# Gated MLP of a two-layer trunk: from a down-projection woven into the up-projection to two phases, with the down-projection in seven products over h kept in DRAM

## The chip, the cores and the metric

The kernel runs on one core of a Trainium2 chip. A core has five engines that run their own instruction lists side by side: TensorE (PE: matmuls, with weight loads, PEld, beside them), VectorE (DVE), ScalarE (ACT), GpSimd (POOL) and SyncE (SP, here only a queue of DMA transfers). They share an on-chip memory, SBUF; matmuls write to eight PSUM banks of 128 × 512 float32. The metric is the time of one execution on the device in microseconds (us): of the kernel before, the median of three runs is 2856.36 us (2855.16 to 2858.88).

## The reference

The reference is a trunk of two layers on x of 1024 positions and 1024 channels. Layer 0 mixes dilated attention with a short convolution, layer 1 is a retention layer; each is followed by a gated MLP with a causal convolution of width 3, which is what the change is about:

```python
def conv_glu_ffn(xn, w_up, conv_w, w_down):
    u = causal_dwconv(xn @ w_up, conv_w)      # 1024 -> 2 x 2816
    g, val = jnp.split(u, 2, axis=-1)
    return (jax.nn.silu(g) * val) @ w_down    # 2816 -> 1024

x = x + conv_glu_ffn(rms_norm(x, ffn_norm[l]), ffn_w_up[l], ffn_conv_w[l], ffn_w_down[l])
```

## The kernel before, in words

**Precision.** Every float32 operand of a large product is kept as a pair of fp32r tiles, high and low (`split`, L99 to L102: ACT casts the high half at L101, another engine subtracts it at L102), and each product is three matmuls (`PASSES`: high × high, high × low, low × high). Weights arrive by SP's queue in `raw` tiles of 128 × 512 (256 KB, L118), of which there are RAW = 3, and become pairs in `hl` tiles, HL = 6. One MLP phase reads the normed x, transposed, from `xc`, which holds the combinations of its halves that the seven products need.

**Up-projection.** The 2816 columns of each half of `w_up` are 22 column blocks of 128 (NFF = 22). `strassen` makes one block: gate and value columns together are a 2 × 2 block product done with seven products instead of eight (Strassen and Winograd). A product is 12 matmuls of 128 × 512 (4 along the contraction, 3 passes), a block 84. They use four PSUM banks x, y, wb, z, from the tags `b`; a `yield` stands behind each product. The weights of the seven products are three blocks of w (11, 12, 22) and four sums of blocks (s1 to s4): DVE adds s1 and s2 (L237, L238), POOL s3 and s4 (L239, L258) and POOL does all seven splits (L102). ACT copies banks out (L245, L261, L266, L272), DVE adds further banks to the copies (L250, L271, L273, L276). The product that comes sixth accumulates once more in bank x and must wait for the copy of x behind the fourth (L261).

**Convolution and gate.** `conv` takes the block's two tiles: ACT multiplies by the third tap (L724), DVE adds the two other taps (L727, two per tile), ACT takes silu (L731), DVE multiplies gate and value (L732), and h is split by ACT and POOL into a pair in SBUF.

**Down-projection.** `down` is a `sweep` over the eight tiles of 128 positions and two halves of the output channels: 16 accumulations of three matmuls each (L289), 48 in a block, and each is added to the residual x in `xb` by DVE (L294). So each of the 22 blocks adds its own share of the down-projection to `xb`: 1056 matmuls and 352 evictions a layer. They use four banks with the tag `o`.

**Order.** The order of emission is written by hand. In `ffn`, `MIX` says how many tiles of the down-projection of the block before are woven in behind each of the seven products of this block. The scheduler keeps the order of PE and may move instructions of the others by their dependencies. The next layer's norm, its transposes and the first block of the next phase (`first_block`, on half-width pieces in all eight banks) are woven by `PLAN` into the sweep of the last block.

Of the kernel before, what the change touches and what calls it, by code (L numbers as in the profile page):

```python
# [9 lines left out]
F32R = mybir.dt.float32r  # L10
# [11 lines left out]
AH = 8  # L22
EPS = 1e-6

RAW = 3
HL = 6

FILL = (1, 2)

PLAN = "s0 q0 s1 q1 r0 t0 s2 q2 c0 r1 t1 s3 q3 c1 r2 t2 c2 r3 h3 t3 c3 h4"  # L30
PLAN_LATE = "t0 c0 s2 q2 t1 s3 q3 c1 r2 t2 c2 r3 t3 h3 c3 h4"
# [37 lines left out]
def trunk(tc, a):  # L69
# [5 lines left out]
    def nm(s):  # L75
        uid[0] += 1
        return f"{s}_{uid[0]}"

    class Pool:


        def __init__(self, name, side="left", space=None):
            kw = {} if space is None else {"space": space}
            self.cm = tc.tile_pool(name=nm(name), bufs=1, side=side, **kw)
            self.p = self.cm.__enter__()

# [108 lines left out]
        for b, t in ((3, t1), (5, t3), (4, t2), (6, t4)):  # L195
            put(b, t, pool)

    def strassen(w, c1, c2, xc, fp, banks, out, spare=None):

        np_ = len(banks)
        width = HALF // np_
        helper = pool if np_ == 1 else dve

        def product(u, hl, b, first=True):
            for k in range(4):
# [16 lines left out]

        def weights(name, src, into=None):
            if name not in hl:
                hl[name] = hilo(src, into, helper)

        for n, bank in enumerate(banks):  # L230
            cols_, ps_ = slice(n * width, (n + 1) * width), n
            if n == 0:
                a11 = col_block(w, c1, 0)
                weights(11, a11)
                a21, a22 = col_block(w, c2, 0), col_block(w, c2, 1)
                s1, s2, s3 = s_tile(), s_tile(), s_tile()
                dve.tensor_tensor(s1, a21, a22, ALU.add)  # L237
# [3 lines left out]
                weights(12, a12)  # L241
                u1, u2 = fp.tile([P, T], "u", 4), fp.tile([P, T], "u", 4)
# [28 lines left out]
            dve.tensor_tensor(half(u2, 1), half(u2, 1), v(x), ALU.add)  # L271
            act.copy(half(u2, 0), v(x))  # L272
            dve.tensor_tensor(half(u2, 0), half(u2, 0), v(wb), ALU.subtract)  # L273
            yield
            product(z, hl["s4"], 2, False)
            dve.tensor_tensor(half(u1, 1), half(u1, 1), v(z), ALU.add)  # L276
# [372 lines left out]
    class Norming:  # L649


        def __init__(self, g):
            self.g = row_gains(g, [wk.tile([P, HALF], "s", 3) for _ in range(2)])
            self.r, self.rows, self.pts = {}, {}, {}

        def play(self, plan, xc=None, sweep=None, head=None):

            for what, n in plan.split():
                n = int(n)
                if what in "sh":
                    for _ in range(2 if what == "s" else n):
                        next(sweep if what == "s" else head)
                elif what == "q":
                    self.r[n] = [
                        inverse_rms(xb[:, t, :], wk.tile([P, T], "s", 3, mybir.dt.bfloat16)) for t in PAIRS[n]
                    ]
                elif what == "r":  # L670
                    self.rows[n] = [normed(xb[:, t, :], r, self.g, u_tile()) for t, r in zip(PAIRS[n], self.r[n])]
                elif what == "t":
                    self.pts[n] = [turn(xn, h, b_bank) for h in range(2) for xn in self.rows[n]]
                else:
                    combine(n, self.pts[n], xc, u_tile(), u_tile())

    def first_block(w, c1, c2, xc):

        us = []

        def spare():
            return h_tile().rearrange("p s (a n) -> p (s a) n", a=2)[:, :2, :]

        return strassen(w, c1, c2, xc, Both, (o_bank, b_bank), us, spare), us

    class Both:
        @staticmethod
# [6 lines left out]
    nrm.play(PLAN, xc, project((6,), ORDER, o_bank), head[0])  # L694


    def ffn(l, xc, head, tail):
# [13 lines left out]
        def wcol(k, j):  # L711
            return cc[:, 44 * k + j : 44 * k + j + 1]

        def conv(j, us, ranges):

            cs = u_tile(), u_tile()
            if len(ranges) == 1:
                h = h_tile()
                h = [h[:, :, :HALF], h[:, :, HALF:]]
            else:  # L720
                h = [wp.tile([P, 2, HALF], "hl", HL, F32R) for _ in ranges]
            for t0, t1 in ranges:
                for jj, u, c in ((NFF + j, us[1], cs[1]), (j, us[0], cs[0])):
                    act.mul(c[:, t0:t1], u[:, t0:t1], wcol(2, jj))  # L724
                    for d in (1, 2):
                        s0 = max(t0, d)
                        dve.scalar_tensor_tensor(  # L727
                            c[:, s0:t1], u[:, s0 - d : t1 - d], wcol(2 - d, jj), c[:, s0:t1], ALU.mult, ALU.add
                        )
                c = cs[0][:, t0:t1]  # L730
                act.activation(c, c, AF.Silu)  # L731
                dve.tensor_tensor(c, c, cs[1][:, t0:t1], ALU.mult)  # L732
                for i in range(t0, t1, HALF):
                    split(h[i // HALF][:, 0], h[i // HALF][:, 1], cs[0][:, i : i + HALF])
            return h

        def down(j, h, tiles, after=None):
            def lhs(s, t):
                return h[t // 4][:, s, t % 4 * P : (t % 4 + 1) * P]

            return sweep([lhs], [w_rows(w_down, j)], tiles, o_bank, after)

        d = iter(())
        for j in range(NFF):
            last = j == NFF - 1
            us = head[1] if j == 0 else []
            steps = head[0] if j == 0 else strassen(w_up, j * P, (NFF + j) * P, xc, Both, (b_bank,), us)
            for n, _ in enumerate(steps):
                for _ in range((MIX, LAST_MIX)[last][n]):
                    next(d, None)  # L750
            if j == 0:
                conv_columns()
            h = conv(j, us, ((0, HALF), (HALF, T)) if last else ((0, T),))
            run(d)
            if not last:
# [236 lines left out]
    def to_out(down):
        run(down(range(NT), lambda t: sync.dma_start(out=a["out"][0, t * P : (t + 1) * P, :], in_=xb[:, t, :])))

    ffn(1, xc, head, to_out)
    close_xc(0, 1, 6, 4, 3, 5, 2)
# [26 lines left out]
```

## Time and profile before

| | us |
|---|---|
| median of three runs | 2856.36 |
| the profiled execution | 2857.22 |
| its span, first to last instruction | 2855.4 |
| PE busy in it | 2743.8 |
| DVE busy | 1802.9 |
| POOL busy | 1553.9 |
| ACT busy | 1101.1 |

The mean granted TensorE clock of the execution is 0.983 of full. PE busy is not PE at its peak: matmuls overlap, so the time of one instruction is longer than the pace at which they follow. The program falls into these stretches (us from the span's start): layer 0's mixer to about 480, the first blocks of its MLP to 625, the steady MLP 625 to 1229, the way to layer 1 (1229 to 1308), the projections of the retention layer and its chunks (1308 to 2110), the way to the second MLP, its steady part 2216 to 2820, and the end. The trace's views by stretch, by line and by chain of waits are shown with the prediction, at the places that use them.

### The profile page before, as it was taken

To read this page: it belongs to the slowest core of one execution; us is meant where nothing else is said; L and a number is where in the kernel's file an instruction comes from. 1 tells how busy PE (TensorE), PEld (TensorE's weight loads), DVE (VectorE), ACT (ScalarE), POOL (GpSimd) and SP (SyncE) were. 2 spreads that over 40 slices of the span, in tenths; PEclk is the share of its full clock that TensorE was granted. 3 is DMA by queue.
4 is the path that set the end of the run, shared out by engine and by line. 5 is a ranking of instruction groups with operands and counts; after the bars stand their busy time and mean duration, and the time that the engine had idled before them with its cause. 6 is when DMAs were issued, how large, how long until landed. Compare 5 with 4: busy or idle time off the path is not lost.

```text
span 2855.4 us, 34163 instructions
## 1 busy us (share of the span) xinstructions
PE 2743.8 (96%) x12513; PEld 2208.3 (77%) x12513; DVE 1802.9 (63%) x2670; ACT 1101.1 (39%) x1860; POOL 1553.9 (54%) x1185
## 2 busy tenths in 40 slices
PE   8999999799999999979999999999997999999998
PEld 6877777578888888867888877788876888888886
DVE  4257665967767767784222224888777767767767
ACT  4355452443333333343333334323344433343342
POOL 6721113465665666546566665555555665665663
PEclk9999999899999999989999999999999999999999
DMA  4310002011111111103333335444221111111112
GB/s 153 103 42 26 24 31 89 23 57 56 48 49 59 49 48 56 49 22 103 112 111 100 109 109 189 147 145 154 83 70 53 48 50 58 49 48 57 51 49 78
DMA packets 214988, 210.84 MB, mean 74 GB/s; under 512 B 10368, under 2 KB 162340, under 8 KB 214820
## 3 DMA queue, kind: packets, MB, share of 16 engines
q1 hardware_dynamic: 207900, 183.49, 20.9%
q10 hardware_dynamic: 6920, 25.17, 2.2%
q8 instruction: 98, 1.61, 0.2%
q14 instruction: 70, 0.57, 0.1%
HBM read 179.26 MB, written 29.36 MB: 73 GB/s over the span
## 4 chain that ended last, share of the span: by engine, by line
PE 76%; DVE 11%; POOL 4%; issue 3%; DMA 3%; ACT 2%; SPq 0%; POOLq 0%; ACTq 0%; DVEq 0%
PE b L210 44%; PE o L289 17%; PE u L419 4%; PE n L368 2%; DVE xb L294 2%; POOL hl L102 2%; PE u L368 2%; PE pv L489 1%; DVE u L164 1%; PE u L289 1%; PE s L458 1%; DMA raw<-in_ret_wo 1%; PE pt L501 1%; DMA raw<-in_ffn_w_up 1%; DVE s L807 1%
## 5 line engine op out<-in xcount | busy, mean ns | idle before, releaser
L210 PE MATMUL b<-xc,hl 128*128 128x512 f32 (+1 forms) x5676 | 1333.1, 393 | 5.8 <-DVE xc L102 2.8
L210 PEld LDWEIGHTS b<-xc,hl 128*128 128x128 f32 x5676 | 1057.2, 189 | 260.0 <-DVE xc L102 3.5
L102 POOL TENSOR_TENSOR hl<-raw,hl 128x512 fp32r<-128x512 f32 x435 | 577.0, 1332 | 862.3 <-ACT hl L101 858.3
L294 DVE TENSOR_TENSOR xb<-xb,o 128x512 f32<-128x512 f32 x880 | 571.7, 683 | 306.3 <-PE o L289 303.5
L101 ACT CAST hl<-raw 128x512 fp32r<-128x512 f32 x444 | 274.2, 620 | 809.7 <-issue 289.2
L289 PE MATMUL o<-hl,h 128*128 128x512 f32 x2112 | 521.0, 398 | 15.4 <-DVE xb L294 11.6
L289 PEld LDWEIGHTS o<-hl,h 128*128 128x128 f32 x2112 | 400.6, 190 | 113.7 <-DVE xb L294 15.5
L102 POOL TENSOR_TENSOR hl<-s,hl 128x512 fp32r<-128x512 f32 x260 | 406.1, 1563 | 107.2 <-ACT hl L101 107.1
L727 DVE SCALAR_TENSOR_TENSOR u<-u,cc,u 128x1023 f32<-128x1023 f32 (+3 forms) x184 | 289.2, 1580 | 7.7 <-ACT u L724 4.9
L101 ACT CAST hl<-s 128x512 fp32r<-128x512 f32 x269 | 165.6, 617 | 89.5 <-PE b L210 40.5
L271 DVE TENSOR_TENSOR u<-u,b 128x512 f32<-128x512 f32 (+1 forms) x68 | 45.9, 675 | 208.6 <-issue 189.2
L419 PE MATMUL u<-xT,hl 128*128 128x512 f32 x576 | 171.2, 413 | 0.0
L237 DVE TENSOR_TENSOR s<-raw,raw 128x512 f32<-128x512 f32 x68 | 52.2, 768 | 137.3 <-DMA raw<-in_ffn_w_up 37.5
L258 POOL TENSOR_TENSOR s<-raw,s 128x512 f32<-128x512 f32 x65 | 126.9, 1953 | 5.1
L724 ACT ACTIVATE u<-u,cc 128x1024 f32<-128x1024 f32 (+1 forms) x92 | 102.0, 1115 | 55.8 <-DVE u L273 31.7
L239 POOL TENSOR_TENSOR s<-raw,raw 128x512 f32<-128x512 f32 x65 | 88.7, 1365 | 54.0 <-DMA raw<-in_ffn_w_up 45.6
L419 PEld LDWEIGHTS u<-xT,hl 128*128 128x128 f32 x576 | 98.2, 189 | 23.3 <-issue 9.3
L102 POOL TENSOR_TENSOR h<-u,h 128x512 fp32r<-128x512 f32 x84 | 106.7, 1290 | 0.0
L289 PE MATMUL o<-hl,ya 128*128 128x512 f32 x384 | 95.4, 397 | 3.7 <-DVE xb L294 3.7
L289 PEld LDWEIGHTS o<-hl,ya 128*128 128x128 f32 x384 | 71.2, 188 | 20.8 <-DVE xb L294 4.6
L102 POOL TENSOR_TENSOR xc<-u,xc 128x512 fp32r<-128x512 f32 x48 | 68.1, 1445 | 35.3 <-ACT xc L101 28.7
L732 DVE TENSOR_TENSOR u<-u,u 128x1024 f32<-128x1024 f32 (+1 forms) x46 | 54.4, 1183 | 49.9 <-ACT u L731 49.9
(183 smaller groups left out, 3040.8 us busy)
## 6 DMA issues: line engine op xcount, KB each, us to landing
raw<-in_ffn_w_up SPq DMA_DIRECT2D x176, 256.0 KB, 2.9
scr<-u ACTq DMA_DIRECT2D x48, 512.0 KB, 4.3
raw<-in_ffn_w_down SPq DMA_DIRECT2D x88, 256.0 KB, 2.7
raw<-in_even_w_in SPq DMA_DIRECT2D x72, 256.0 KB, 2.8
raw<-in_ret_wo SPq DMA_DIRECT2D x64, 256.0 KB, 2.7
xb<-in_x SPq DMA_DIRECT2D x16, 512.0 KB, 4.2
raw<-in_ret_wv SPq DMA_DIRECT2D x32, 256.0 KB, 4.1
raw<-in_ret_wg SPq DMA_DIRECT2D x32, 256.0 KB, 3.4
```

The source lines that it names most:

```text
L101: act.copy(hi, src)
L102: (eng or pool).tensor_tensor(lo, src, f(hi), ALU.subtract)
L210: pe.matmul(u, hl[:, ws, k * P : (k + 1) * P], xc[b][:, xs, k, cols_], start=(first and k == 0 and i == 0), stop=(k == 3 and i == 2), skip ...
L239: helper.tensor_tensor(s3, a11, a21, ALU.subtract)
L258: helper.tensor_tensor(s4, a12, s2, ALU.subtract)
L289: pe.matmul(o, lhs[j](ls, t), ws[j][hf][:, w, :], start=(j == 0 and i == 0), stop=(j == n - 1 and i == 2),)
L294: dve.tensor_tensor(xs, xs, o, ALU.add)
L368: pe.matmul(banks[t], xT[:, xs, k, t0 : t0 + P], hl[:, ws, :], start=(k == 0 and i == 0), stop=(k == KT - 1 and i == 2),)
L419: pe.matmul(u, hl(ws, k), xT[:, xs, k, hf * 512 : (hf + 1) * 512], start=(k == 0 and i == 0), stop=(k == KT - 1 and i == 2),)
L724: act.mul(c[:, t0:t1], u[:, t0:t1], wcol(2, jj))
L727: dve.scalar_tensor_tensor(c[:, s0:t1], u[:, s0 - d : t1 - d], wcol(2 - d, jj), c[:, s0:t1], ALU.mult, ALU.add)
L732: dve.tensor_tensor(c, c, cs[1][:, t0:t1], ALU.mult)
```

## The change

**Two phases.** In each MLP all 22 blocks of the up-projection run first, alone. h is no longer split in SBUF; each block's h (128 × 1024 float32, 512 KB) is stored to DRAM (`hs`, L901, on ACT's DMA queue), after the second product of the next block. The blocks take the four `b` and the four `o` banks by turns.

**Down-projection in seven products.** `down_steps` treats w_down and h as 2 × 2 blocks: h by halves of the 2816 channels and halves of the 1024 positions, w_down by halves of its rows and of its output channels. Groups 12, 56 and 37 each do two of the seven products: 11 steps (KH = 11) of 24 matmuls into all eight banks. Groups 4 and 4b do the last one in two halves, 11 steps of 6 matmuls each. That is 924 matmuls a layer and 28 evictions (L834). Rows of h are read back once, in group 12 (L735, two of 512 KB a step), and stay in SBUF; sums are formed in place (L758). The combination t4 goes to DRAM from group 4 (`ts`, L809) and is read again, with a quarter of h, into raw tiles in group 4b (L814, L815). Loads run four steps ahead (LOADS), splits two (AHEAD).

**Engines.** In a full-width block only the splits of 11, 12 and 22 stay on POOL. The other four splits and the sums s3 and s4 move to DVE, and so do all splits and sums of the down phase.

**Around it.** RAW goes from 3 to 5, HL from 6 to 7; tiles wait for a tile's reuse, not a slot's neighbours (`reuse_waits="tile"`); the gains of a norm have a tag of their own; the first block hands its steps out by one more yield. `PLAN_DOWN` weaves the norm and the first block of the retention layer into groups 4 and 4b of MLP 0, with the position tiles in another pairing (`lay=1`). At the end `to_out` stores tiles of the output between the steps of groups 4 and 4b.

Lines move: L102 becomes L110, L210 becomes L220, L250 L264, L261 L275, L271 L285, L272 L286, L276 L290, L289 L303 (attention and retention only), L724 L890, L727 L892, L731 L893, L732 L894.

```diff
-RAW = 3
-HL = 6
+RAW = 5
+HL = 7
+KH = NFF // 2
+AHEAD = 2
+LOADS = 4
-MIX = (0, 0, 0, 0, 3, 3, 2)
-LAST_MIX = (0, 0, 0, 0, 3, 0, 0)
...
-        helper = pool if np_ == 1 else dve
+        subs = {11: pool, 12: pool, 22: pool} if np_ == 1 else {}
...
-                hl[name] = hilo(src, into, helper)
+                hl[name] = hilo(src, into, subs.get(name, dve))
...
-                helper.tensor_tensor(s3, a11, a21, ALU.subtract)
+                dve.tensor_tensor(s3, a11, a21, ALU.subtract)
...
-                helper.tensor_tensor(s4, a12, s2, ALU.subtract)
+                dve.tensor_tensor(s4, a12, s2, ALU.subtract)
...
+        def make_12(k, b11, b21):
+            a11, a21, a12, a22 = (t[k][:, i * HALF : (i + 1) * HALF] for t in (left, right) for i in range(2))
+            p1 = both(a11), both(b11)
+            s1 = kept[k] = pools[k >= 3].tile([P, HALF], "s1", 3 if k < 3 else KH - 3)
+            add(s1, a21, a22, ALU.add)
+            p2 = both(a12), both(b21)
+            add(a21, a11, a21, ALU.subtract)
+            return [p1, p2]
...
+        def load_4b(k):
+            t4, a22 = raw(), raw()
+            sync.dma_start(out=t4, in_=ts[k])
+            sync.dma_start(out=a22[:, :256], in_=hs[KH + k, :, HALF + 256 : T])
+            return t4, a22
...
+        groups = (
+            (load_12, make_12, [(x, four, True), (y, four, True)], [(y, 0, 0), (x, 0, 0)]),
+            (load_56, make_56, [(y, four, True), (x, four, False)], [(y, 4, 1), (x, 0, 1)]),
+            (load_37, make_37, [(y, four, False), (x, four, False)], [(y, 0, 1), (x, 4, 1)]),
+            (load_4, make_4, [(x[:2], two, False)], [(x[:2], 4, 0)]),
+            (load_4b, make_4b, [(x[2:], two, False)], [(x[2:], 6, 0)]),
+        )
...
         for j in range(NFF):
-            last = j == NFF - 1
             us = head[1] if j == 0 else []
-            steps = head[0] if j == 0 else strassen(w_up, j * P, (NFF + j) * P, xc, Both, (b_bank,), us)
+            steps = head[0] if j == 0 else strassen(
+                w_up, j * P, (NFF + j) * P, xc, Both, ((o_bank, b_bank)[j % 2],), us, lay=lay
+            )
             for n, _ in enumerate(steps):
-                for _ in range((MIX, LAST_MIX)[last][n]):
-                    next(d, None)
+                if n == 2:
+                    store()
+                if j == NFF - 1 and n >= 3:
+                    if n == 3:
+                        close_xc(0, 1)
+                        d.append(down_steps(w_down))
+                    advance(1)
             if j == 0:
                 conv_columns()
-            h = conv(j, us, ((0, HALF), (HALF, T)) if last else ((0, T),))
-            run(d)
-            if not last:
-                d = down(j, h, range(NT))
+            held.append((j, conv(j, us)))
+        advance(2)
+        store()
+        tail(until, d[0])
```

**Three places in the engines' instruction lists.** A row gives the line, the operation, what it writes and, after `<-`, what it reads; the numbers tell buffers apart.

ACT in a steady block of the MLP, before: from the copy of bank x behind the first product (L245) to the copy of x for which the sixth product waits (L261).

```order
L245 COPY u_5771<-b_5773 128x2x256
L101 CAST hl_5821<-s_5760 128x512
L731 ACTIVATE u_5726<-u_5726 128x1024
L101 CAST hl_5839<-s_5762 128x512
L101 CAST h_5728<-u_5726 128x512 x2
L101 CAST hl_5855<-s_5824 128x512
L261 COPY u_5771<-b_5773 128x2x256
```

The same stretch of ACT after the change, between the copies L259 and L275:

```order
L259 COPY u_5814<-b_5816 128x2x256
L109 CAST hl_5957<-raw_5955 128x512
L893 ACTIVATE u_5784<-u_5784 128x1024
L109 CAST hl_5979<-raw_5947 128x512
L901 DMA hs_5386<-u_5784 128x1024
L275 COPY u_5814<-b_5816 128x2x256
```

The two casts of h are gone; in their place stands the store of h, directly ahead of the copy of x, and the casts between are those of weights of the next block, no longer of this one.

DVE in a steady block before: the sums of weights and of banks, with evictions of the down-projection (L294) among them.

```order
L294 TENSOR_TENSOR xb_71<-xb_71,o_5883 128x512
L237 TENSOR_TENSOR s_6000<-raw_5996,raw_5998 128x512
L238 TENSOR_TENSOR s_6001<-s_6000,raw_5991 128x512
L271 TENSOR_TENSOR u_5772<-u_5772,b_5773 128x2x256
L294 TENSOR_TENSOR xb_71<-xb_71,o_5903 128x512
L273 TENSOR_TENSOR u_5772<-u_5772,b_5775 128x2x256
```

DVE in a steady block after, from the third weight sum to the sum of the sixth product (L285):

```order
L251 TENSOR_TENSOR s_5951<-raw_5940,raw_5945 128x512
L892 SCALAR_TENSOR_TENSOR u_5784<-u_5668,cc_5388,u_5784 128x1022
L264 TENSOR_TENSOR u_5814<-u_5814,b_5817 128x2x256
L894 TENSOR_TENSOR u_5784<-u_5784,u_5785 128x1024
L110 TENSOR_TENSOR hl_5995<-s_5950,hl_5995 128x512
L110 TENSOR_TENSOR hl_6010<-s_5949,hl_6010 128x512
L272 TENSOR_TENSOR s_6013<-raw_5955,s_5950 128x512
L249 TENSOR_TENSOR s_6095<-raw_6091,raw_6093 128x512
L285 TENSOR_TENSOR u_5815<-u_5815,b_5816 128x2x256
```

The evictions are gone; four splits (L110) and the sums s3 and s4 (L251, L272) stand between the convolution's steps, the gate product (L894) and the sums of banks.

SP's queue near the end of the program, after (before it ended with the eight stores of the output in a row): loads of group 4b from `ts` and `hs`, with stores of the output between them.

```order
L814 DMA raw_22797<-ts_5387 128x512
L1175 DMA out<-xb_71 128x1024 x4
L1175 DMA out<-xb_71 128x512 x2
L815 DMA raw_22798<-hs_5386 128x256
L814 DMA raw_22813<-ts_5387 128x512
L815 DMA raw_22814<-hs_5386 128x256
L814 DMA raw_22833<-ts_5387 128x512
L815 DMA raw_22834<-hs_5386 128x256
L814 DMA raw_22849<-ts_5387 128x512
L1175 DMA out<-xb_71 128x1024
```

Loads of later steps now stand in the queue behind stores, which wait for the evictions of their tiles.

More of the change, by code (lines that the diff above doesn't have):

```diff
@@ L649, in trunk, with __init__ @@
     class Norming:
-        def __init__(self, g):
-            self.g = row_gains(g, [wk.tile([P, HALF], "s", 3) for _ in range(2)])
+        def __init__(self, g, lay=0):
+            self.g = row_gains(g, [wk.tile([P, HALF], "g", 2) for _ in range(2)])
+            self.pairs = PAIRS[lay]
             self.r, self.rows, self.pts = {}, {}, {}
@@ L662, in play, with first_block @@
                 n = int(n)
-                if what in "sh":
+                if what in "sdh":
                     for _ in range(2 if what == "s" else n):
[L665 to L671, printed above, removed]
+                        next(head if what == "h" else sweep)
+                elif what in "qab":
+                    for i in {"q": (0, 1), "a": (0,), "b": (1,)}[what]:
+                        t = self.pairs[n][i]
+                        self.r[t] = inverse_rms(xb[:, t, :], wk.tile([P, T], "s", 3, mybir.dt.bfloat16))
+                elif what in "rAB":
+                    for i in {"r": (0, 1), "A": (0,), "B": (1,)}[what]:
+                        t = self.pairs[n][i]
+                        self.rows[t] = normed(xb[:, t, :], self.r[t], self.g, u_tile())
                 elif what == "t":
-                    self.pts[n] = [turn(xn, h, b_bank) for h in range(2) for xn in self.rows[n]]
+                    self.pts[n] = [turn(self.rows[t], h, b_bank) for h in range(2) for t in self.pairs[n]]
                 else:
                     combine(n, self.pts[n], xc, u_tile(), u_tile())
-    def first_block(w, c1, c2, xc):
+    def first_block(w, c1, c2, xc, lay=0):
         us = []
@@ L682, in spare @@
             return h_tile().rearrange("p s (a n) -> p (s a) n", a=2)[:, :2, :]
-        return strassen(w, c1, c2, xc, Both, (o_bank, b_bank), us, spare), us
+        return strassen(w, c1, c2, xc, Both, (o_bank, b_bank), us, spare, lay), us
     class Both:
@@ L712, in wcol, with conv @@
             return cc[:, 44 * k + j : 44 * k + j + 1]
-        def conv(j, us, ranges):
+        def conv(j, us):
             cs = u_tile(), u_tile()
[L717 to L743, printed above, removed]
+            for jj, u, c in ((NFF + j, us[1], cs[1]), (j, us[0], cs[0])):
+                act.mul(c, u, wcol(2, jj))
+                for d in (1, 2):
+                    dve.scalar_tensor_tensor(c[:, d:], u[:, :-d], wcol(2 - d, jj), c[:, d:], ALU.mult, ALU.add)
@@ new lines, in conv, with store, advance, until @@
+            act.activation(cs[0], cs[0], AF.Silu)
+            dve.tensor_tensor(cs[0], cs[0], cs[1], ALU.mult)
+            return cs[0]
+        held = []
+        def store():
+            for j, h in held:
+                act.dma_start(out=hs[j], in_=h)
+            held.clear()
+        done = [0]
+        def advance(n):
+            for _ in range(n):
+                next(d[0])
+            done[0] += n
+        def until(g):
+            advance(LOADS + g * KH - done[0])
+        d = []
@@ L767, in trunk, with to_ret @@
-    ffn(0, xc, head, to_ret)
-    dp = Pool("dp", space=bass.MemoryType.DRAM)
+            held.append((j, conv(j, us)))
+        advance(2)
+        store()
+        tail(until, d[0])
+    nxt = {}
+    def to_ret(until, down):
+        until(3)
+        nrm = Norming(a["odd_norm"][0:1], 1)
+        nrm.play(PLAN_DOWN[0], sweep=down)
+        open_xc()
+        nxt["xc"] = xc_tiles()
+        nxt["head"] = first_block(a["ret_wq"][0], 0, P, nxt["xc"], 1)
+        nrm.play(PLAN_DOWN[1], nxt["xc"], down, nxt["head"][0])
@@ L943, in trunk @@
         us = [] if n else nxt["head"][1]
-        steps = strassen(w, c0, c0 + P, xc, Both, (b_bank,), us) if n else nxt["head"][0]
+        steps = strassen(w, c0, c0 + P, xc, Both, ((b_bank, o_bank)[n % 2],), us, lay=1) if n else nxt["head"][0]
         run(steps if n + 1 < len(pairs) else last_block(steps))
@@ L991, in trunk, with to_out, put @@
     nrm.play(PLAN_LATE, xc, wo_sweep(half, h, yT, 1, ORDER[4:]), head[0])
[L994 to L998, printed above, removed]
+    def to_out(until, down):
+        def put(t, cs=slice(0, D)):
+            sync.dma_start(out=a["out"][0, t * P : (t + 1) * P, cs], in_=xb[:, t, cs])
+        until(3)
+        next(down)
+        next(down)
+        for t in range(4):
+            put(t)
+            next(down)
+        for t in (6, 7):
+            put(t, slice(HALF, D))
+        for _ in range(5):
+            next(down)
+        next(down)
+        next(down)
+        for t in (4, 5):
+            put(t)
+        run(down)
+        for t in (6, 7):
+            put(t, slice(0, HALF))
+    ffn(1, xc, head, 0, to_out)
     for p in (ps, dp, wk, mp, sm, xp, wp, cp):
```

127 lines of the change are left out of this document (116 added, 11 removed).

## The prediction

> **What bounds the kernel now.** I read the page first (busy time by engine, then the costliest groups), then busy time by stretches, then the chain of waits, and last the timeline of one block.
>
> ```profile
> span 2855.4 us, 34163 instructions
> ...
> PE 2743.8 (96%) x12513; PEld 2208.3 (77%) x12513; DVE 1802.9 (63%) x2670; ACT 1101.1 (39%) x1860; POOL 1553.9 (54%) x1185
> ...
> GB/s 153 103 42 26 24 31 89 23 57 56 48 49 59 49 48 56 49 22 103 112 111 100 109 109 189 147 145 154 83 70 53 48 50 58 49 48 57 51 49 78
> ...
> L294 DVE TENSOR_TENSOR xb<-xb,o 128x512 f32<-128x512 f32 x880 | 571.7, 683 | 306.3 <-PE o L289 303.5
> ...
> L289 PE MATMUL o<-hl,h 128*128 128x512 f32 x2112 | 521.0, 398 | 15.4 <-DVE xb L294 11.6
> ```
> ```profile
> 480.00:625.00 145.00, 119.78 (x582) 97.92 (x581) 109.43 (x147) 54.54 (x95) 65.65 (x56) 0.92 0.14 41
> 625.00:1229.00 604.00, 604.00 (x2588) 486.68 (x2587) 422.70 (x524) 230.75 (x353) 378.45 (x255) 1.00 0.17 52
> 1229.00:1308.00 79.00, 55.40 (x267) 46.47 (x266) 70.97 (x100) 38.66 (x71) 38.49 (x38) 0.78 0.07 20
> 1308.00:1654.00 346.00, 346.00 (x1514) 279.76 (x1513) 85.87 (x109) 123.93 (x209) 213.97 (x159) 1.00 0.33 110
> ...
> 1753.00:2110.00 357.00, 343.75 (x1657) 284.27 (x1657) 287.78 (x451) 116.74 (x206) 194.22 (x184) 0.98 0.43 141
> ...
> 2216.00:2820.00 604.00, 604.00 (x2589) 487.01 (x2588) 423.87 (x526) 231.40 (x354) 378.73 (x255) 1.00 0.17 51
> 2820.00:2855.00 35.00, 26.54 (x102) 20.54 (x100) 26.34 (x40) 6.80 (x11) 5.04 (x4) 0.87 0.30 121
> ```
>
> A row of the second view gives the stretch, its length, then the busy time of PE, weight loads, DVE, ACT and POOL, the granted clock, the DMA share and GB/s. TensorE is busy in all of the two stretches of 604 us, which hold most of the two gated MLPs, at full clock; DVE has 70% there, POOL 63%. So inside an MLP only fewer matmuls, or cheaper ones, can save time; between the MLPs (1229:1308) PE idles and DVE, 90% busy, sets the pace.
>
> ```profile
> 717.79 14.04 PE b L210 x60
> 731.84 4.18 PE o L289 x18
> ...
> 748.61 14.04 PE b L210 x60
> ...
> 1229.03 5.63 PE b L210 x24
> ...
> 1299.59 8.22 PE o L210 x68
> 1307.81 345.83 PE b L210 x1512
> ...
> 2819.79 5.63 PE b L210 x24
> ```
>
> These are pieces of the chain of waits (start, length, what; u, hl, s, xb, raw are tiles named in the kernel). A block of the MLP takes 748.61 − 717.79 = 30.82 us for 84 up matmuls (b, L210) and 48 down ones (o, L289). The price of a matmul is its pace: 14.04/60 = 0.234 us up, 4.18/18 = 0.2322 us down. The page's mean of 398 ns is one matmul's length with its pipeline: 264 of them would be 105 us by it, 61 by the pace. I take the pace.
>
> **The change part by part.** The sum is against the profiled execution, 2857.2 us (span 2855.4), which lies 0.9 above the median of 2856.4.
>
> 1. *Down-projection in seven products.* Per layer 55 group-steps: 33 with 24 matmuls (groups 12, 56, 37) and 22 with 6 (groups 4 and 4b): 924 instead of 1056 (half of the group's x2112). −264 × 0.2322 = **−61.3 us**, if PE stays full. The 880 evictions shrink with them, off the path in the 604 us stretches.
>
> 2. *The up phase alone.* A block is now 84 × 0.234 = 19.7 us instead of 30.8, with nearly all of DVE's, ACT's and POOL's work of a block pressed into it.
>
> ```profile
> 713.29 2.60 DVE L727 SCALAR_TENSOR_TENSOR u<-u,cc,u 128x1023 f32<-128x1023 f32 x2
> ...
> 715.79 1.29 POOL L102 TENSOR_TENSOR hl<-raw,hl 128x512 fp32r<-128x512 f32 x1 [5.69 <-ACT hl L101]
> ...
> 718.79 4.07 DVE L727 SCALAR_TENSOR_TENSOR u<-u,cc,u 128x1023 f32<-128x1023 f32 x2
> 719.51 4.51 POOL L102 TENSOR_TENSOR hl<-s,hl 128x512 fp32r<-128x512 f32 x2
> 719.58 0.34 SPq L118 DMA_DIRECT2D raw<-in_ffn_w_down  x1
> ```
> ```profile
> L724 ACT ACTIVATE u<-u,cc 128x1024 f32<-128x1024 f32 x84 | 96.7, 1153 | 54.1 <-DVE u L273 30.2 <-DVE u L276 23.8
> ...
> L732 DVE TENSOR_TENSOR u<-u,u 128x1024 f32<-128x1024 f32 x42 | 51.5, 1226 | 49.9 <-ACT u L731 49.9
> ...
> L731 ACT ACTIVATE u<-u 128x1024 f32<-128x1024 f32 x42 | 44.5, 1061 | 40.7 <-DVE u L727 40.6
> ...
> L276 DVE TENSOR_TENSOR u<-u,b 128x512 f32<-128x512 f32 x65 | 44.4, 683 | 17.3 <-PE b L210 17.2
> L272 ACT COPY u<-b 128x512 f32<-128x512 f32 x65 | 38.1, 587 | 30.4 <-DVE u L271 23.6
> L102 DVE TENSOR_TENSOR xc<-b,xc 128x512 fp32r<-128x512 f32 x36 | 24.5, 682 | 0.0
> ```
> ```profile
> 584.61 0.70 DVE s L237
> ```
>
> Two DVE convolution steps alone take 2.60, a POOL split alone 1.29. Side by side they take 5.23 together (718.79 to 724.02), which is 2.60 + 2 × 1.29 = 5.18: they took turns. The Trainium skill, "SBUF — State Buffer", "Who interferes with whom", says that a DVE instruction with two SBUF inputs and a GpSimd one reading SBUF hold a shared port in turn, each for its whole length; the rows agree, and by it the two engines' work adds. DVE per block: 4 weight adds at 0.70 and 4 splits at 0.68, 4 sums with PSUM at 0.68, 4 convolution steps at 1.30, one product at 1.23 = 14.7 us. POOL: 3 × 1.29 = 3.9. Even added, 18.6 is under 19.7. ACT: 7 casts and 4 copies at about 0.6, two products at 1.15, a silu of 1.06 = 10. So the throughput fits, with 1.1 us over.
>
> The latency is tighter. Counted from the end of a block's last product (time 0): last sum with PSUM 0.25 to 0.95; ACT's product to 2.15; meanwhile on DVE, in its order, step, split, step, step, weight add, step: 4 × 1.30 + 0.68 + 0.70 = 6.6, ending at 7.5; silu to 8.6, gate product to 9.9. Behind it on ACT stand, in this order, the store of h (L901), which waits for the gate product, and the copy of bank x (L275). The sixth product of the next block accumulates in x again and waits for that copy: due at 60 × 0.234 = 14.0. Without collisions the copy ends at 10.6; with the three POOL splits all in DVE's way, 10.6 + 3.9 = 14.5. Part of them falls beside the silu and PSUM sum, so I take 13.6: on time by 0.4. Weights are a block ahead, so their delay is absorbed. Bounds: 0 to +0.85 us per block (the 18.6 plus the waits for silu and for the hand-overs, 20.5), so 0 to +36 over 42 blocks. I take **+6**, near the lower end, since the sum of work fits. The store itself: before, the 512 KB stores of the retention phase (scr, below) stood on ACT while PE ran 346 us without a gap.
>
> 3. *First block of an MLP.*
>
> ```profile
> 586.83 6.74 PE L210 MATMUL b<-xc,hl 128*128 128x512 f32 x26
> ...
> 624.92 1.33 PE L210 MATMUL b<-xc,hl 128*128 128x512 f32 x5
> ```
>
> In PE's timeline block 1 of layer 0 takes 624.92 − 586.83 = 38.1, 7.3 over the steady 30.8: weights come late, POOL being full. Now four splits are on DVE and two more raw tiles are there. I leave 2.3 per layer: **−10** for two layers (bounds 0 and −14.6).
>
> 4. *Down phase.* A step of 24 matmuls is 5.57 us. DVE: 6 or 7 operations at about 0.69, 4.1 to 4.8; ACT 4 casts, 2.5; POOL is idle, so nothing takes turns. Both fit. Group 12 also reads 2 × 512 + 2 × 256 KB in each 5.57 us: 282 GB/s.
>
> ```profile
> 10.00:20.00 10.00, 7.21 (x26) 5.58 (x25) 7.70 (x9) 8.27 (x17) 6.80 (x10) 1.00 0.95 362
> ```
> ```profile
> scr<-u ACTq DMA_DIRECT2D x48, 512.0 KB, 4.3
> raw<-in_ffn_w_down SPq DMA_DIRECT2D x88, 256.0 KB, 2.7
> ...
> out<-xb SPq DMA_DIRECT2D x8, 512.0 KB, 2.7
> ```
>
> Busy queues moved 362 GB/s at the start of the program, so 78% is wanted. Loads run four steps ahead. I take nothing here, and +3 per layer at the entry (the last convolution shares DVE with the first splits; bounds 0 and 7). Steps of group 4b are 6 × 0.2322 = 1.39 us, but need two of five raw tiles each; a tile is held for issue 0.34, load 2.7, cast 0.6, split 0.7 = 4.3, so 4.3/2.5 = 1.74 a step: (11 − 2.5) × 0.35 = +3 (by 4.3 a load, as for scr, +9).
>
> 5. *From MLP 0 to retention.*
>
> ```profile
> 1269.13 2.82 PE L171 MATMUL b<-ident,u 128*128 128x128 f32 x12 [2.17 <-DVE u L164]
> ...
> 1299.38 7.02 PE L210 MATMUL o<-xc,hl 128*128 128x256 f32 x56
> ```
>
> Before, from 1229.03 + 5.63 = 1234.7 to 1307.8: 73.1 us for 78 down matmuls (18.1), 64 transposes at 2.82/12 (15.0) and 168 half-width matmuls at 7.02/56 (21.0), together 54.1: 19 lost. Now groups 4 and 4b run beside the norm: 132 × 0.2322 + 36 = 66.7 for PE. DVE: 71.0 less 26 evictions (17.8) and the last convolution (9.5) is 43.7; plus 12 evictions (8.2) and 22 steps at 1.05 (split 0.68, half split 0.37) is 75. DVE still sets the pace; I take 80 with its hand-overs, so 13.3 lost and 3 at the entry: **−3** (bounds −8 and +7).
>
> 6. *End.* Before, from 2825.4 to 2855.4: 30.0 with 18.1 of matmuls, 11.9 lost. Now 3 (entry) + 3 (4b) + two evictions and the hand-over 1.6 + a store of at most 2.7 (out, x8) + 1 behind other stores on SP's queue = 11.3: **0**, within ±5.
>
> 7. *More raw and hl tiles elsewhere.* Stretch 1753:2110 loses 13.3 us, partly to weight loads. **−3**, bounds 0 and −10. Moving two adds of retention's blocks from POOL to DVE costs nothing: PE never waited there (346.00 busy of 346) and DVE has 260 us to spare.
>
> Sum: −61.3 + 6 − 10 − 3 + 0 − 3 = −71.3, so **2786 us**.
>
> **The rivals.**
> - *R1: the order of ACT and DVE sets the up phase.* The copy of x comes after 14.0. For it: 0.4 us of margin, and POOL splits that grew to 2.25 each beside DVE (719.51, 4.51 for two). Against: the summed work fits. 20.3 us a block, +0.65 × 42 = 27 instead of 6: **2807**; at its bound of 20.5, 2816.
> - *R2: the down phase waits for DRAM.* For it: 282 GB/s of reads, with stores before them in the queues, and none of the page's 40 slices of 71 us (the GB/s row) ran above 189. At 230 GB/s a step of group 12 is 6.8 us: 11 × 1.25 × 2 = 27, less what the lead of four steps hides (4): **2809**. Below it stands the clock: TensorE got 0.78 in 1229:1308, where it waited. The Trainium skill, "TensorE: Matmul & The Clock Gate", "HAM oscillation — how this bites in real kernels", says that idle gaps over about 3.4 us throttle the clock; waits of 1.25 us would not.
> - *R3: slower than before.* The store of h stands ahead of the copy on ACT; if that copy ended 5.4 us later than the 10.6 (at 16.0), each block would last 21.7, and 42 × 2.0 = 84 us instead of 6 would be spent: **2864**. That is the point from which it decides. For it: POOL's mean of operations beside DVE rises, and each collision delays a chain whose every link is in order. Against: it needs DVE to lose 5 us of 19.7 to 3.9 us of POOL work.
> - *R4: the change does not do what it says*: waits take back all of the 61 + 10 us, 0.65 on each of 110 group-steps: 2857. It would need every step to wait, where only those of 12 and 4b are near a limit.
>
> **How the numbers follow.** Forecast 2763 to 2800: 0.58. R1 0.23, R2 0.11, R3 0.06, R4 0.02. Lowest: −61.3 − 14.6 − 8 − 10, 2763. Highest, without more than 2 in 10 left out: R1 at its bound with part of R2, 2825. A measurement of this kernel tells 0.2% from no change, 5.7 us; faster by more 0.91, within 0.02, slower 0.07.
>
> **What would show it.** A block of the up phase of 19.7 us, as one piece of the chain, confirms step 2; pieces of 60 and 24 matmuls broken by ACT's copy at L275 or the store's predecessor L894 show R1 or R3, by their period. The down matmuls (L826) at 0.232 confirm step 1. PE waits for rows of h in group 12, and DMA near its limit there, show R2. A stretch between MLP 0 and retention with DVE near full confirms step 5; idle time before L826 with raw tiles as releaser, 4b. I am wrong if the up block is over 20.5, or group 12's steps over 6.5.

## The result and the profile after

The changed kernel takes 2763.76 us (median of four runs, 2762.86 to 2764.28), the kernel before 2855.76 in the same sitting: a ratio of 0.968, with a 95% interval of 0.966 to 0.969. The forecast was 2786, its range 2763 to 2825. The profiled execution has a span of 2761.1 us against 2855.4, 94.3 less; the forecast's sum was 71.3 less.

The page of the kernel after, in the form shown for the kernel before (an engine's busy time; then line, engine, operation, tiles, count, busy time and mean ns; then DMA issues with size and time to landing):

```profile
span 2761.1 us, 33920 instructions
...
PE 2675.4 (97%) x12249; PEld 2151.1 (78%) x12249; DVE 1953.2 (71%) x2930; ACT 1191.6 (43%) x2030; POOL 754.2 (27%) x619
...
L892 DVE SCALAR_TENSOR_TENSOR u<-u,cc,u 128x1022 f32<-128x1022 f32 (+1 forms) x176 | 303.2, 1744 | 1.1
...
L826 PE MATMUL o<-hl,hl 128*128 128x512 f32 x444 | 110.7, 393 | 2.4 <-DVE hl L110 1.6
...
hs<-u ACTq DMA_DIRECT2D x44, 512.0 KB, 2.7
h<-hs SPq DMA_DIRECT2D x44, 512.0 KB, 5.9
```

POOL's time is halved, DVE has 150 us more, and PE's share has risen from 96 to 97%. By stretches, after (same columns as before; the cuts are the start of block 1 of each MLP, the first down matmul, the end of group 37, and the start of the retention's block 1):

```profile
586.83:1000.58 413.75, 413.65 (x1766) 332.26 (x1765) 332.02 (x363) 201.60 (x296) 98.98 (x60) 1.00 0.27 87
1000.58:1186.76 186.18, 183.41 (x794) 148.26 (x793) 153.88 (x247) 80.93 (x142) 1.22 (x4) 1.00 0.54 184
1186.76:1268.99 82.23, 67.58 (x370) 54.99 (x368) 72.61 (x113) 49.11 (x101) 37.02 (x32) 0.94 0.29 87
...
2125.13:2539.00 413.87, 413.73 (x1766) 332.36 (x1766) 330.68 (x362) 200.50 (x295) 100.42 (x60) 1.00 0.28 87
2539.00:2724.60 185.60, 183.45 (x794) 148.18 (x793) 154.54 (x247) 78.55 (x137) 0.00 (x0) 1.00 0.56 190
2724.60:2761.00 36.40, 31.64 (x133) 24.29 (x131) 22.75 (x44) 16.49 (x35) 0.00 (x0) 1.00 0.52 178
```

Both up phases keep PE busy to within 0.15 us of 414, at full clock; both down phases lose under 3 us. The chain of waits says the same of the up phase, block after block:

```profile
607.14 19.68 PE o L220 x84
626.82 19.68 PE b L220 x84
...
961.38 19.69 PE o L220 x84
...
989.73 8.96 DMA hs<-u
...
1002.79 5.40 DMA h<-hs
...
2737.83 3.17 DMA raw<-hs
```

h's way through DRAM stands on the chain at two places only: at the entry of each down phase, where a late store and a first read are on it, and beside groups 4 and 4b, where t4 and a quarter of h are read again (once in MLP 0, three times near the end).

Cut at the same four places, the spans of the profiled executions (each is one execution; the first column runs from 581.0 to 586.8 between the profiles of kernels that do not differ from the one after up to there):

| us | to MLP 0 block 1 | MLP 0 to retention | retention to MLP 1 | MLP 1 to the end |
|---|---|---|---|---|
| before | 586.8 | 729.3 | 863.8 | 675.5 |
| before, RAW 5 and HL 7 (`e6_before_raw5`) | 584.5 | 718.9 | 856.6 | 670.5 |
| after, RAW 3 and HL 6 (`e5_raw3`) | 588.9 | 722.5 | 865.5 | 675.6 |
| after | 586.8 | 682.2 | 856.1 | 636.0 |

Each MLP gained 40 to 47 us and the retention layer, whose code is nearly unchanged, 7.6.

### The profile page after: what moved, and what is told of

Same layout as the page of the kernel before. It is cut to its first block, busy times and chain, and to the rows that moved or that the text cites. A ratio compares the mean times of both kernels' runs of the same rounds, so it can differ in the third digit from the quotient of the medians.

```text
span 2761.1 us, 33920 instructions
## 1 busy us (share of the span) xinstructions
PE 2675.4 (97%) x12249; PEld 2151.1 (78%) x12249; DVE 1953.2 (71%) x2930; ACT 1191.6 (43%) x2030; POOL 754.2 (27%) x619
## 4 chain that ended last, share of the span: by engine, by line
PE 75%; DVE 12%; POOL 5%; issue 3%; DMA 3%; ACT 2%; SPq 0%; DVEq 0%; POOLq 0%; ACTq 0%
PE o L220 23%; PE b L220 22%; PE o L826 7%; PE b L826 6%; PE u L433 4%; PE n L382 2%; PE u L382 2%; PE o L303 2%; POOL hl L110 2%; DVE xb L308 2%; PE pv L503 1%; PE u L303 1%; PE s L472 1%; PE pt L515 1%; DVE u L172 1%
## 5 line engine op out<-in xcount | busy, mean ns | idle before, releaser
L110 POOL TENSOR_TENSOR hl<-raw,hl 128x512 fp32r<-128x512 f32 x347 | 499.3, 1448 | 1316.7 <-ACT hl L109 1293.4
L220 PE MATMUL b<-xc,hl 128*128 128x512 f32 (+1 forms) x2988 | 684.1, 388 | 1.4 <-POOL xc L110 0.9
L220 PE MATMUL o<-xc,hl 128*128 128x512 f32 (+1 forms) x2904 | 672.8, 391 | 10.3 <-ACT u L275 3.0
L220 PEld LDWEIGHTS b<-xc,hl 128*128 128x128 f32 x2988 | 548.5, 188 | 130.2 <-POOL xc L110 1.2
L220 PEld LDWEIGHTS o<-xc,hl 128*128 128x128 f32 x2904 | 537.9, 191 | 136.9 <-ACT u L275 3.6
L110 DVE TENSOR_TENSOR hl<-s,hl 128x512 fp32r<-128x512 f32 x325 | 225.1, 696 | 359.1 <-ACT hl L109 359.1
L109 ACT CAST hl<-raw 128x512 fp32r<-128x512 f32 (+1 forms) x424 | 257.9, 612 | 428.7 <-PE o L303 79.5
L892 DVE SCALAR_TENSOR_TENSOR u<-u,cc,u 128x1022 f32<-128x1022 f32 (+1 forms) x176 | 303.2, 1744 | 1.1
L308 DVE TENSOR_TENSOR xb<-xb,o 128x512 f32<-128x512 f32 x176 | 114.9, 678 | 21.9 <-PE o L303 21.6
L890 ACT ACTIVATE u<-u,cc 128x1024 f32<-128x1024 f32 x88 | 101.1, 1151 | 38.5 <-DVE u L287 30.2
L826 PE MATMUL o<-hl,hl 128*128 128x512 f32 x444 | 110.7, 393 | 2.4 <-DVE hl L110 1.6
L303 PE MATMUL o<-hl,ya 128*128 128x512 f32 x384 | 97.8, 406 | 5.1 <-DVE xb L308 5.1
L893 ACT ACTIVATE u<-u 128x1024 f32<-128x1024 f32 x44 | 46.7, 1062 | 110.3 <-DVE u L892 110.2
L303 PEld LDWEIGHTS o<-hl,ya 128*128 128x128 f32 x384 | 73.4, 194 | 22.2 <-DVE xb L308 5.4
L303 PE MATMUL o<-hl,yb 128*128 128x512 f32 x336 | 81.2, 397 | 0.0
L110 POOL TENSOR_TENSOR xc<-u,xc 128x512 fp32r<-128x512 f32 x48 | 66.4, 1411 | 35.7 <-DVE u L199 19.8
```

Source lines behind the costliest of these rows:

```text
L109: act.copy(hi, src)
L110: (eng or pool).tensor_tensor(lo, src, f(hi), ALU.subtract)
L220: pe.matmul(u, hl[:, ws, k * P : (k + 1) * P], xc[b][:, xs, k, cols_], start=(first and k == 0 and i == 0), stop=(k == 3 and i == 2), skip ...
L303: pe.matmul(o, lhs[j](ls, t), ws[j][hf][:, w, :], start=(j == 0 and i == 0), stop=(j == n - 1 and i == 2),)
L308: dve.tensor_tensor(xs, xs, o, ALU.add)
L826: pe.matmul(o, l[:, ls, c * P : (c + 1) * P], r[:, ws, :], start=(start and i == 0), stop=(stop and i == 2), skip_group_check=True,)
```

## The experiments

**How much room has the up block?** In one block of the kernel after (timeline: start, length, engine, line):

```profile
705.38 19.84 PE L220 MATMUL b<-xc,hl 128*128 128x512 f32 x84
...
708.20 3.52 DVE L892 SCALAR_TENSOR_TENSOR u<-u,cc,u 128x1022 f32<-128x1022 f32 x2
...
709.13 1.50 POOL L110 TENSOR_TENSOR hl<-raw,hl 128x512 fp32r<-128x512 f32 x1 [10.68 <-ACT hl L109]
...
715.75 1.23 DVE L894 TENSOR_TENSOR u<-u,u 128x1024 f32<-128x1024 f32 x1 [0.59 <-ACT u L893]
...
717.01 0.33 ACTq L901 DMA_DIRECT2D hs<-u  x1
717.38 0.59 ACT L275 COPY u<-b 128x512 f32<-128x512 f32 x1 [1.15 <-DVE u L894]
```

The first matmul of the block starts at 705.38; the copy of bank x ends at 717.97, 12.6 later, where 13.6 was forecast and 14.06 (60 matmuls at 19.68/84) is the limit. So 1.5 us are spare. Two kernels lengthen just this chain on ACT, by copying h onto itself ahead of its store: once in `e3_pad1`, whose edit follows, and three times in `e4_pad3`, with `range(3)`.

```diff
             for j, h in held:
+                for _ in range(1):
+                    act.copy(h, h)
                 act.dma_start(out=hs[j], in_=h)
```

> After, with one more pass of ACT over h (a copy in place, 128x1024, about 1.1 us) between the gate product and the store, so ahead of the copy of bank x in every up block. Theory (that copy has 1.5 us to spare in after: it ends 12.5 us after the block's start and is due at 14.06): block 19.68, 2764 within 5. Rival (the chain gate product, store, copy already paces the block): +1.1 x 42 = +46, 2810.

> As e3_pad1 with three copies, of which the instruction order puts two ahead of the copy of bank x. Theory (1.5 us to spare, then each us counts in each block): 2.3 - 1.5 = 0.8 us a block, block 20.5, +34 over 42 blocks, 2798 (2785 to 2815). Rival (the order of ACT does not matter, PE always has other work): 2764 within 5.

With one copy: 2768.2 us (2765.2 to 2771.1), and the up phases take 413.8 and 414.4 us, nearly as after (413.8); the copy of x ends 13.7 us into a block. What the profile has more is behind the up phase of MLP 0, above all in one wait of PE, 4.2 us between the first two groups of the down phase, where after waits 1.0; whether the copies cause it is not shown. With three: 2772.2 us, up phases 419.0 and 418.8, most blocks 19.8 to 20.1. The timeline of `e4_pad3`:

```profile
781.53 20.02 PE L220 MATMUL b<-xc,hl 128*128 128x512 f32 x84
...
783.60 6.94 DVE L892 SCALAR_TENSOR_TENSOR u<-u,cc,u 128x1023 f32<-128x1023 f32 x4
...
792.87 1.79 DVE L251 TENSOR_TENSOR s<-raw,raw 128x512 f32<-128x512 f32 x1
792.99 2.13 ACT L902 COPY u<-u 128x1024 f32<-128x1024 f32 x2 [0.79 <-DVE u L894]
795.03 0.57 ACT L275 COPY u<-b 128x512 f32<-128x512 f32 x1
795.50 1.05 ACT L902 COPY u<-u 128x1024 f32<-128x1024 f32 x1
795.65 5.45 PEld L220 LDWEIGHTS b<-xc,hl 128*128 128x128 f32 x24 [0.35 <-ACT u L275]
...
796.58 0.33 ACTq L903 DMA_DIRECT2D hs<-u  x1
```

The copy ends 14.07 us after 781.53, and there PE first waits for it: the limit is where it was worked out, and the mechanism of R1 and R3 is real. Of the price expected, 0.8 us a block, only 0.25 came on average, because the scheduler answered: the issue of the store now stands behind the third copy, no longer ahead of the copy of x (717.01 in the kernel after), and with the four convolution steps in one row the gate product ends 11.4 us into a block instead of 11.6. So two copies of 2.13 us together moved the copy of x by 1.5. A chain on paper is lengthened less than by what is added when its order is free to change.

**Does it matter that the splits moved to DVE?**

In `e2_pool` all seven splits and the sums s3 and s4 are on POOL again:

```diff
-        subs = {11: pool, 12: pool, 22: pool} if np_ == 1 else {}
+        helper = pool if np_ == 1 else dve
...
-                hl[name] = hilo(src, into, subs.get(name, dve))
+                hl[name] = hilo(src, into, helper)
...
-                dve.tensor_tensor(s3, a11, a21, ALU.subtract)
+                helper.tensor_tensor(s3, a11, a21, ALU.subtract)
...
-                dve.tensor_tensor(s4, a12, s2, ALU.subtract)
+                helper.tensor_tensor(s4, a12, s2, ALU.subtract)
```

In `e7_all_dve` nothing of this is on POOL:

```diff
-        subs = {11: pool, 12: pool, 22: pool} if np_ == 1 else {}
+        subs = {}
```

> After, but in full-width blocks all seven splits and the sums s3 and s4 are on POOL, as in the kernel before. Theory (DVE operations with two SBUF inputs and POOL's take turns): DVE 7.8 us of such work, POOL 9 x 1.29 = 11.6, together 19.4 of 19.68 us with waits on top; block 20.5 to 23 us, 2800 to 2900 in all. Rival (POOL's work hides beside DVE's, as the 346 us of retention without a gap in the kernel before suggest): block 19.68, 2764 within 5.

> After with the last three splits of a full-width block (11, 12, 22) moved from POOL to DVE too, so that POOL does nothing in the up phase. Theory (DVE and POOL take turns on operations with two SBUF inputs): the convolution steps (L892) fall from a mean of 1.75 us to about 1.30, DVE has 14.7 + 3 x 0.68 = 16.7 us of 19.7, block 19.68, total 2764 within 6. Rival (POOL is not what lengthens them): the mean stays above 1.6, DVE has 18.5 us, and the block may pass 19.68.

`e2_pool`: 2813.7 us, over half of the gain gone. Its timeline, PE and the copy for which PE waits:

```profile
814.52 8.59 PE L220 MATMUL o<-xc,hl 128*128 128x512 f32 x36
...
823.00 0.59 ACT L259 COPY u<-o 128x512 f32<-128x512 f32 x1 [2.76 <-DVE u L892]
...
823.64 11.91 PE L220 MATMUL o<-xc,hl 128*128 128x512 f32 x48 [0.53 <-ACT u L259]
...
835.38 8.59 PE L220 MATMUL b<-xc,hl 128*128 128x512 f32 x36
```

Each block takes 20.86 us: 1.18 × 42 = 50, which is the whole difference. PE waits here for another copy of x than the one that the prediction watched: L259, behind the first product, for which the fourth product waits (11.5 and 11.2 us in the two up phases). That copy in turn waited 2.76 us for a convolution step, L892; both use tiles u, of which there are four.

`e7_all_dve`: 2757.8 us (2756.6 to 2760.5), 6 less than after. That is no gain of the up phases, which PE paces in both: they take 413.4 us instead of 413.8. Of the 4.6 us between the profiles, 3.4 lie ahead of MLP 0, where the code is the same. The convolution step L892 in a stretch of the up phase of MLP 0, first after, then `e7_all_dve` (min/median/max ns):

```profile
L892 DVE SCALAR_TENSOR_TENSOR u<-u,cc,u x64: 1275/1798/2326, 647.4 to 948.4; 128x1023 f32<-128x1023 f32 x32, 128x1022 f32<-128x1022 f32 x32
```
```profile
L892 DVE SCALAR_TENSOR_TENSOR u<-u,cc,u x65: 1272/1278/1285, 643.6 to 958.5; 128x1023 f32<-128x1023 f32 x33, 128x1022 f32<-128x1022 f32 x32
```

With POOL silent every step takes 1.28 us; with three POOL splits in a block some take up to 2.33. So POOL's work lengthens DVE's. That they take turns, and do not share evenly, shows in the first timeline above, under the question of room: the split at 709.13 lasts 1.50 us, little over the 1.29 that it takes alone, while the two convolution steps beside it (708.20) take 3.52 instead of 2.60. The Trainium skill ("SBUF — State Buffer", "Who interferes with whom") says the same of a DVE operation with two SBUF inputs and a GpSimd one that reads SBUF. A split takes 1.29 us alone on POOL and 0.68 on DVE, so moving it saves time for both: from 605 to 995 us DVE is busy 306.6 us in `e7_all_dve` and 314.3 after, though it does all splits.

The way to retention was tried with the opposite move, one split of each group 4b step from DVE to POOL.

```diff
-    def down_steps(w):
+    def down_steps(w, eng4b=dve):
...
-            return [(quarter(a22[:, :256]), both(t4))]
+            return [(quarter(a22[:, :256]), both(t4, eng4b))]
...
-                        d.append(down_steps(w_down))
+                        d.append(down_steps(w_down, (pool, dve)[l]))
```

> After with the 128x512 split of each group 4b step of MLP 0 on POOL instead of DVE (11 splits), on the way to retention, where PE loses 15.5 us and DVE is busy 72.6 of 82.2 us while POOL has 37. Theory (the engines take turns, so moving such work to POOL, where it takes 1.29 instead of 0.68 us, adds to the sum of both): 0 to 8 us slower, 2764 to 2772. Rival (DVE alone is the bound there and 7.5 us leave it): 4 to 8 us faster, 2756 to 2760.

2763.0 us (2761.4 to 2764.2); MLP 0 to retention 682.9 us against 682.2. Nothing gained, as turn-taking has it, though this alone could also be chance.

**Does it matter that there are two bank sets?**

```diff
-                w_up, j * P, (NFF + j) * P, xc, Both, ((o_bank, b_bank)[j % 2],), us, lay=lay
+                w_up, j * P, (NFF + j) * P, xc, Both, (b_bank,), us, lay=lay
```

> After with one bank set: every full-width up block uses the four b banks. Theory (the 19.68 us block is bound by its 84 matmuls): the banks are free in time, since in the trace of after the copy that frees x (L286) ends 0.9 us before the last product does; block 19.68 us, total 2764 within 5. Rival (the two sets carry part of the gain): each block waits 0.5 to 2 us for its first bank, 2785 to 2848.

2759.9 us (2756.4 to 2763.5), up phases 413.85 and 413.78. The alternation carries nothing of the gain.

**What do the deeper tiles carry?**

> After with RAW = 3 and HL = 6 as in the kernel before. Theory (the deeper tiles carry most of what retention and the MLPs' first blocks gained, and group 4b needs them): retention's 5.7 us of PE waits come back, a few us at the first blocks, and each step of 4b takes 4.3/1.5 = 2.9 us instead of 1.4, +16 at the end and some at the way to retention: 2784 to 2800. Rival (the depth hardly matters, since loads are issued far ahead): 2764 within 6.

> The kernel before with RAW = 5 and HL = 7 alone. Theory (the deeper tiles, not the work moved to DVE, carry the gains outside the MLPs' steady parts): retention -6, first blocks of the MLPs -4 to -10 of the 12.6 us that they lose, 2840 to 2848. Rival (those gains come from the splits and sums moved from POOL to DVE): 2856 within 4.

The kernel before with RAW 5 and HL 7: 2831.8 us, ratio 0.992 (0.991 to 0.994), 22 us gained without any of the rest, more than either theory said (8 to 16, and none). The kernel after with RAW 3 and HL 6: 2859.7 us (2854.3 to 2867.4), ratio 1.002: no gain left. The theory named the direction and missed the size by 60 us, since it looked for the loss outside the up phase. Half of it is inside, 435.9 and 436.7 us instead of 413.8; the rest is where it looked, 18.2 and 16.7 us behind the two up phases and 9.4 in the retention. Why the up phase is slower shows in the timeline of `e5_raw3`:

```profile
704.23 0.69 DVE L251 TENSOR_TENSOR s<-raw,raw 128x512 f32<-128x512 f32 x1
704.98 21.81 SPq L126 DMA_DIRECT2D raw<-in_ffn_w_up  x6
...
708.06 1.14 ACT L109 CAST hl<-raw 128x512 fp32r<-128x512 f32 x2 [3.36 <-DMA raw<-in_ffn_w_up]
...
709.10 0.58 ACT L280 COPY u<-o 128x512 f32<-128x512 f32 x1
...
709.73 3.07 PE L220 MATMUL o<-xc,hl 128*128 128x512 f32 x12 [0.86 <-ACT u L280]
```

A load waits until the sum L251 has read its raw tile; the cast of the weights it brings stands on ACT, in order, ahead of the copy L280; the last product waits for that copy. So a late load of the next block's weights stops this block: PE waits for L280 in 17 blocks of each up phase. The two numbers apart:

> After with RAW = 3 alone, HL = 7 kept. Theory (a block needs four raw tiles, and the fourth load waits for a split; in e5 the block was 20.85 us and its chain went through a load in every block): block 20.8, 2840 to 2860. Rival (the pairs, HL, set e5's pace): block 19.68, 2764 to 2790.

> After with HL = 6 alone, RAW = 5 kept. Theory (raw tiles were e5's limit; six pairs for seven products still let a pair be made one product ahead of a whole block): block 19.68, 2764 to 2775. Rival (HL was e5's limit): block over 20.5, 2820 or more.

> After with RAW = 4. Theory (four raw tiles are one block's loads, so the up block keeps 19.68; group 4b has 4.3/2 = 2.15 us a step instead of 1.39): up phase unchanged, +8 at the end and up to +8 on the way to retention, 2770 to 2782. Rival (the fifth tile is what puts loads a block ahead): block over 20 us, 2785 or more.

| after, with | us | up phases |
|---|---|---|
| RAW 3, HL 7 (`e9_raw3_hl7`) | 2854.8 (2849.3 to 2862.5) | 440.8, 440.3 |
| RAW 4, HL 7 (`e11_raw4`) | 2773.8 (2771.9 to 2775.6) | 413.7, 413.8 |
| RAW 5, HL 7 (after) | 2763.8 (2762.9 to 2764.3) | 413.8, 413.8 |
| RAW 5, HL 6 (`e10_raw5_hl6`) | 2754.2 (2753.6 to 2754.8) | 413.4, 413.4 |

It is the raw tiles. Three cost all; with three and seven pairs PE waits mostly at the copy L275, the one that R1 named (12.6 and 12.2 us in the two up phases), but for want of raw tiles. Four, a block's loads, keep the up phase at PE's pace. The fifth pays in the down phase: the last stretch, from MLP 1 on, is 644.1 us with four and 636.0 with five. The expectation put this down to group 4b and met the total by luck: of the 8.1 us, 2.4 lie in groups 4 and 4b and 5.7 in the groups before. The largest loss there stands at the start of group 56 of `e11_raw4`:

```profile
2605.68 5.46 PE L826 MATMUL b<-hl,hl 128*128 128x512 f32 x12 [4.38 <-ACT u L109]
```

PE waits 4.4 us there, and the product behind the wait takes 5.46 us, where it took 3.00 after (2602.95).

The seventh pair is not needed; without it the kernel is the fastest of all that ran, by 9.6 us under after in two runs, and 10 below what was expected. The profile has 3.4 of it between the start of MLP 0 and retention, 1.7 in MLP 1 and 4.1 ahead of MLP 0, where profiles scatter by as much. In both down phases group 12 is shorter, 61.3 us instead of 64.6 and 64.0, without after's waits at the entry; why was not found.

Last, the change's division of work in the old, interleaved order:

```diff
-RAW = 3
-HL = 6
+RAW = 5
+HL = 7
...
+        subs = {11: pool, 12: pool, 22: pool} if np_ == 1 else {}
...
-                hl[name] = hilo(src, into, helper)
+                hl[name] = hilo(src, into, subs.get(name, dve))
...
-                helper.tensor_tensor(s3, a11, a21, ALU.subtract)
+                dve.tensor_tensor(s3, a11, a21, ALU.subtract)
...
-                helper.tensor_tensor(s4, a12, s2, ALU.subtract)
+                dve.tensor_tensor(s4, a12, s2, ALU.subtract)
```

> The kernel before with RAW = 5, HL = 7 and with the change's division of splits and sums (11, 12, 22 on POOL, the rest on DVE) in its interleaved blocks. Theory (a block is 30.8 us of matmuls, DVE's part grows from 21.5 to about 25.6 us and stays under it): block 30.82, total as e6_before_raw5, 2832 within 5. Rival (evictions on DVE come later behind the splits, and PE waits for its o banks): block over 31, 2838 or more.

2826.0 us (2824.8 to 2827.1), 6 under `e6_before_raw5` and a little below what was expected; the block is 30.82 us as before (L290 x18 at 690.32 and at 721.14), and 3.2 of the 5.5 us between the two profiles lie in the retention. While 48 down matmuls cover each block, its pace does not depend on who splits; once they are gone, it does (`e2_pool`).

No run has the two phases without the seven products, or the seven products in the old order. What each is worth rests on counts of matmuls and their pace.

## Why the prediction came out as it did

The direction and the main term were right; the size was 23 us short on the span, from seven terms that nearly all erred to the same side. The time lies 0.8 us above the lower end of the range, which was the sum of the terms at their best: that it lies inside is in part luck.

- *Step 1, the matmuls.* Forecast −61.3. Confirmed in kind: from `e6_before_raw5` to after, with equal tile depths, the span falls by 69.4 us, nearly all in the MLPs. The down matmuls run at 13.81/60 = 0.2302 us (1070.90 to 1084.71 in the chain) instead of 0.2322, so 490.4 − 425.4 = 65.0 in place of 61.3.
- *Step 2, the up phase.* Forecast 19.7 us of matmuls and +0.15 a block, +6 in all; measured 19.68 and nothing. The copy of x came at 12.6, not 13.6, since less of POOL's work fell in DVE's way. R1 and R3 did not occur, but their mechanism holds: `e4_pad3` brought it about at this copy, and `e2_pool`, with more of POOL's work in DVE's way, at an earlier one.
- *Step 3, the first blocks.* Before, they lost 7.3 and 5.3 us over 30.8 (2179.86 to 2215.97 in the second MLP); after, 20.2 against 19.7. −11.6 against a forecast of −10.
- *Step 4, the down phase.* The waits at the entry end 15 us in. R2 did not occur: while PE did group 12 (1000.58 to 1065.14) the queues moved 261 GB/s (282 were reckoned), PE was busy in 61.8 of the 64.6 us, and after this row it ran without a wait to the end of the group:

```profile
1015.60 3.06 PE L826 MATMUL o<-hl,u 128*128 128x512 f32 x12 [0.90 <-ACT u L109]
```

  33 steps at 5.52 are 182.2 of the 186.2 us, so the entry, with a wait of 1.0 for evictions between two groups (at 1065.14), cost 4.0 (forecast 3). Group 4b kept 1.39 us a step up to its last three, which came 1.4 us late in all (forecast 3).
- *Step 5, the way to retention.* Here a row was misread. 1307.81 is the start of a chain piece that begins with 72 half-width matmuls of the first block; the retention's block 1 starts at 1316.1:

```profile
1307.64 7.21 PE L210 MATMUL b<-xc,hl 128*128 128x256 f32 x60
1314.69 1.57 PE L210 MATMUL b<-xc,h 128*128 128x256 f32 x12
1316.09 34.13 PE L210 MATMUL b<-xc,hl 128*128 128x512 f32 x145
```

  So the kernel before lost 81.4 − 54.1 = 27.3 us there, not 19. After, 82.2 us against a forecast of 80, with DVE busy in 72.6 of it (forecast 75) and 15.8 lost beside 30.4 + 36.0 of work at the measured pace. With the entry −7.5 instead of −3. Two errors are in it and partly cancel: 8.3 too little for what was lost before, and 3.5 too little for what is lost after.
- *Step 6, the end.* 11.9 lost before, 9.5 after; −2.4 instead of 0.
- *Step 7, the tiles.* Forecast −3 in the retention layer, measured −7.6; `e6_before_raw5` puts 7.2 of it on RAW and HL. What the prediction did not see is that the depth is more than a term of its own: step 2 rested on "weights are a block ahead", and with three raw tiles that sentence is false, which costs 22 to 27 us in each up phase, half of the gain; the other half goes where the down phases and the retention lack the tiles. No rival named it.

These add up to −65.0 + 0 − 11.6 − 7.5 − 2.4 − 7.6 = −94.1, of the 94.3 measured.

## What to carry to other kernels

When work that covered a loop is taken out of it, look for what the cover hid: the loop's pace is then set by the latest in-order operation that stands ahead of a copy PE waits for, and here that could be a copy put behind the gate product, a convolution step that took turns with POOL, or a load that waited for a raw tile. The number of buffers belongs to the schedule: five raw tiles and a seventh pair instead of three and six were worth 22 us to the old one and 96 to the new, where the raw tiles alone are worth 91. Before a stretch's loss is summed, check in the engine's own timeline that a merged piece of the chain starts where the next phase does.

## What was not expected of the hardware

The price of a product of 12 matmuls of 128x512 with the same three passes is 2.81 us in the up phase (19.68/7) and 2.76 on average in the down phase (13.81/5); in the down phase's timeline products follow one another at 2.72 to 2.80 us. No run tells why. A long wait of PE cost more than its length: behind the 4.4 us in `e11_raw4` the granted clock was 0.50 for the next product (2605.68 to 2611.10), while behind a wait of 1.0 us (1065.14 after) it stayed at 1.00. And the two kernels of the new order with three raw tiles scattered over 13 us between runs (ten and eight of them), while the kernel before, with three raw tiles too, stayed within 6.3 in 13 runs. Why is open too.
